# Deferring the factors and biases of five DeepNorms in a two-layer encoder trunk

## The chip, the core and the metric

One core of one Trainium2 chip. The metric is the device time of one execution in microseconds; times of several executions are given by their median. TensorE (PE in the profile, PEld for its weight loads) multiplies, VectorE (DVE), ScalarE (ACT) and GpSimd (POOL) work elementwise, SyncE (SP) issues most transfers. Each engine runs its own instructions in order and waits for the others by semaphores.

## The reference, cut to what matters

512 tokens of 1024 features go through two layers. Layer 0 is FFN, mLSTM mixer, FFN, embedding gate; layer 1 is FFN, gMLP mixer, FFN, embedding gate. After each of the eight parts stands a post-normalisation of `ALPHA * x + part`, over the features of a token:

```
def layer_norm(x, g, b):
    mu = jnp.mean(x32, axis=-1, keepdims=True)
    var = jnp.mean(jnp.square(x32 - mu), axis=-1, keepdims=True)
    y = (x32 - mu) * lax.rsqrt(var + LN_EPS) * g + b
...
x = layer_norm(DN_ALPHA * x + 0.5 * swiglu_ffn(x, ...), ln_g[i, 0], ln_b[i, 0])
x = layer_norm(DN_ALPHA * x + mix, ln_g[i, 1], ln_b[i, 1])
x = layer_norm(DN_ALPHA * x + 0.5 * swiglu_ffn(x, ...), ln_g[i, 2], ln_b[i, 2])
ple = jax.nn.sigmoid(x @ ple_wg[i] + ple_bg[i]) * (p[i] @ ple_wp[i])
x = layer_norm(DN_ALPHA * x + ple, ln_g[i, 3], ln_b[i, 3])
```

All of it is float32. The result is the normalised x of the last part.

## The kernel before

The state `xt` stands in the core's memory by tokens: four tiles t of 128 tokens with 1024 features each. Products need x by features, so each tile is turned: `turn_x` transposes it on PE in halves of four 128x128 blocks, ScalarE copies the half rounded to the short format (`xh`, line 419), and DVE subtracts to get the low part (`xl`, line 420). Every product is three matmuls, high times high, high times low and low times high (`mm3`, lines 250 to 254). Weights are split the same way: class `Weights` loads raw tiles through SP's queue, ScalarE makes `whi` (line 182) and DVE `wlo` (line 183), or GpSimd where a caller gives `low=pool`. A fixed order of all splits (`W.order`) is worked down as buffers come free: `release` gives one back and calls `fill`; with `later=True` it is only noted in `W.held`, and `refill` frees it. There are four buffers of the kind main; stages open more (`rows`, `extra`). `take` hands the next split tile to a product, and calls `refill` where none is ready.

The order of the work on each engine is the order of the program text. A stage ends with a `down` product: for each token tile t it adds into two PSUM banks (of four, `dn_bank`), over the n parts of the hidden state. Behind it DVE adds the result to `xt` (`residual`, lines 516 to 521: L519 for the first addition, which also scales by ALPHA, L521 for the others), takes the statistics (L500), and `Norm.apply` (lines 502 to 514) follows for the tile before, at k = 1 of the next tile. `apply` is: mean and variance (L505), plus eps (L507), GpSimd's power -0.5 (L508), and for each half of the features two scalar_tensor_tensor passes, subtract the mean and multiply by the factor (L511), multiply by the reciprocal deviation and add the bias (L512). The factor and bias stand in `g_bc` and `b_bc`, spread over all partitions. Tiles 0 and 1 are turned inside the down product (lines 548 and 549); tiles 2 and 3 in four hooks, which the next stage calls between its matmuls. The last hook (`last_turn`) also calls `W.refill(4)`.

The next stage starts with `up_staged` (lines 581 to 599) where it is an FFN or the mLSTM: three products over tokens 0 to 255 first, with the four hooks inside the second and third, then the same three over tokens 256 to 511, whose first product needs tiles 2 and 3. The gMLP starts with products by token tile (line 1047), with hooks ahead of and inside each, and takes four weight tiles for the first of them. In an FFN (`ffn`, line 665) the hidden features come in chunks of 2, 4, 4, 4, 4, 4 blocks; each block takes two steps i, a Silu (L701) and a product (L707). The first chunk's `down` stands at chunk 1, step 1 (line 715), with n = 2. In the mLSTM, value tiles are made by token tile (`project_v`, line 866), with the gates' scan (L801) and its transposes (L813, L815) between them. The embedding stage (`ffn_ple`, line 1134) computes a gate by tokens (lines 1186 to 1212) with the norm of each tile in `rest`.

Of the kernel before, what the change touches and what calls it, by code (L numbers as in the profile page):

```python
# [9 lines left out]
F32 = mybir.dt.float32  # L10
F32R = mybir.dt.float32r
AF = mybir.ActivationFunctionType
OP = mybir.AluOpType
# [208 lines left out]
def hybrid_trunk(ctx: ExitStack, tc, x, p, ln_g, ln_b, ffn1_wgu, ffn1_wd, ffn2_wgu, ffn2_wd,  # L222
# [188 lines left out]
    def turn_x(t, bank=dn_bank, halves=(0, 1)):  # L411

        for g in halves:
# [4 lines left out]
            dst = (slice(None), slice(4 * g, 4 * g + 4), slice(t * P, (t + 1) * P))  # L418
            sca.activation(xh[dst], ps, AF.Copy)
# [3 lines left out]
    NCOL = 160  # L423
# [3 lines left out]
    def load_columns():  # L427
# [6 lines left out]
                ("vn_b", gm_vn_b[0].rearrange("(a c) -> a c", c=P))]  # L434
# [52 lines left out]
    class Norm:  # L487
        def __init__(self, layer, k, out=None):
            self.out, self.st = out, {}
# [12 lines left out]
        def apply(self, t):  # L502
            y = xt[:, t]
# [5 lines left out]
            mean, rstd = mv[:, 0:1], rs[:, 1:2]  # L509
            for c in (slice(0, 512), slice(512, D)):  # L510
                vec.scalar_tensor_tensor(y[:, c], y[:, c], mean, self.g_bc[:, c], op0=OP.subtract, op1=OP.mult)  # L511
                vec.scalar_tensor_tensor(y[:, c], y[:, c], rstd, self.b_bc[:, c], op0=OP.mult, op1=OP.add)  # L512
                if self.out is not None:
                    nc.sync.dma_start(self.out[0, t * P:(t + 1) * P, c], y[:, c])

# [8 lines left out]
    hooks = []  # L524
# [5 lines left out]
    def last_turn():  # L530
        turn_x(TB - 1, halves=(1,))
        W.refill(4)

    def set_hooks():
        hooks.extend([lambda: turn_x(TB - 2, halves=(0,)), lambda: turn_x(TB - 2, halves=(1,)),
                      lambda: turn_x(TB - 1, halves=(0,)), last_turn])

    def down(hs, first, norm=None, low=None):

        n = len(hs)  # L540
        ws, kinds = [], []
        for t in range(TB):
            banks = [dn_bank("dps"), dn_bank("dps")]
            for k in range(n):
# [3 lines left out]
                if norm is not None and k in (1, 2) and t >= 2:  # L548
                    turn_x(t - 2, up_bank, (k - 1,))
                if norm is not None and k == 1 and t:  # L550
                    norm.apply(t - 1)
# [4 lines left out]
                if t == TB - 1:  # L556
                    kind = "rows" if kinds[k] == "rows" else None
                    if norm is None:
                        W.release(kind=kind, low=low)
                    elif kind == "rows":  # L560
                        W.free[kind] += 1
                    else:
                        W.release(later=bool(W.held), low=pool)
                        if not W.held:
                            W.held.append("none")
# [4 lines left out]
        if norm is not None:  # L570
            norm.apply(TB - 1)
            set_hooks()
# [92 lines left out]
    def ffn(layer, k, rows, prepare=None):  # L665
        with stage_pool("forms", 2) as fpool, stage_pool("quarters", Q_BUFS) as qpool, stage_pool("hpool", 2) as hpool:
# [16 lines left out]
            for c, n in enumerate(FFN_CHUNKS):  # L683
# [10 lines left out]
                for i in range(2 * n):  # L694
# [17 lines left out]
                    if group is not None and i < 7:  # L712
                        group.product(i)
                        group.form()
# [541 lines left out]
```

## Time and profile before

| | |
|---|---|
| median of 3 runs | 2289.18 us (2288.74 to 2290.45) |
| the profiled execution | 2285.76 us |
| its span, first to last instruction | 2284.0 us |
| PE busy | 2239.8 us |
| DVE busy | 1495.8 us |
| ACT busy | 784.2 us |
| POOL busy | 206.4 us |

The profile has times in us from the start of the span, durations of groups as a mean in ns. A wait is put down to the instruction that came last by the profile. PE's matmuls are pipelined, so the duration of one (about 0.39 us for 128x512) is longer than the step from one to the next. [...]

### The profile page before, as it was taken

What the parts mean: (1) busy time and instruction counts of PE and PEld (TensorE: products, weight loads), DVE (VectorE), ACT (ScalarE), POOL (GpSimd) and SP (SyncE); (2) the same over time, 40 slices, a digit from 0 to 9 for tenths busy, and PEclk for the clock granted to TensorE, in tenths of its full rate; (3) what the DMA queues carried; (4) which work ended last, traced back from release to release, by engine and by line L of the source; (5) the groups of instructions that cost most, each with busy time, mean ns of one, the idle gap of its engine ahead of it and who ended that gap; (6) DMA issues with size and microseconds to landing.
All of it is one profiled execution on the core that took longest, in us unless ns stands there. A gap on an engine that the chain in (4) does not pass through costs nothing.

```text
span 2284.0 us, 26044 instructions
## 1 busy us (share of the span) xinstructions
PE 2239.8 (98%) x10622; PEld 1873.3 (82%) x10622; DVE 1495.8 (65%) x2093; ACT 784.2 (34%) x1032; POOL 206.4 (9%) x143
## 2 busy tenths in 40 slices
PE   8999999999999999999999999999999999999997
PEld 7888888887878788888878888888888888888886
DVE  4566659676666656666687566668566674666677
ACT  3333333442534123333243233333333332333332
POOL 1000002132232300000010000001021210000010
PEclk9999999999999999999999999999999999999999
DMA  7332222133231333331332333222322243332212
GB/s 232 113 98 86 93 86 95 48 114 110 66 102 56 120 111 120 111 96 62 111 120 88 112 105 111 93 70 95 131 93 86 75 133 113 129 111 83 83 65 74
DMA packets 172848, 228.30 MB, mean 100 GB/s; under 512 B 4788, under 2 KB 130836, under 8 KB 172728
## 3 DMA queue, kind: packets, MB, share of 16 engines
q1 hardware_dynamic: 165824, 211.83, 28.6%
q10 hardware_dynamic: 6616, 14.69, 2.0%
q8 instruction: 83, 1.36, 0.2%
q14 instruction: 37, 0.30, 0.0%
q0 software_dynamic: 288, 0.12, 0.0%
HBM read 224.51 MB, written 2.11 MB: 99 GB/s over the span
## 4 chain that ended last, share of the span: by engine, by line
PE 82%; DVE 12%; issue 2%; POOL 2%; ACT 1%; DMA 1%; POOLq 0%; SPq 0%; ACTq 0%; DVEq 0%
PE fps L253 13%; PE fps L254 13%; PE fps L252 13%; PE gps L253 4%; PE gps L254 4%; PE gps L252 4%; PE dps L253 3%; PE dps L254 3%; PE dps L252 3%; DVE wlo L183 2%; DVE xt L512 2%; DVE st L500 1%; PE gups L252 1%; PE vps L252 1%; PE gups L253 1%
## 5 line engine op out<-in xcount | busy, mean ns | idle before, releaser
L252 PE MATMUL fps<-xh,whi 128*128 128x512 f32 x1312 | 510.6, 389 | 0.0
L253 PE MATMUL fps<-xl,whi 128*128 128x512 f32 x1312 | 510.4, 389 | 0.0
L254 PE MATMUL fps<-xh,wlo 128*128 128x512 f32 x1312 | 510.4, 389 | 0.0
L183 DVE TENSOR_TENSOR wlo<-wraw,whi 128x1024 fp32r<-128x1024 f32 (+1 forms) x274 | 336.0, 1242 | 199.2 <-ACT whi L182 197.4
L182 ACT ACTIVATE whi<-wraw 128x1024 fp32r<-128x1024 f32 (+1 forms) x333 | 344.1, 1048 | 263.3 <-PE dps L254 126.2
L252 PEld LDWEIGHTS fps<-xh,whi 128*128 128x128 f32 x1312 | 246.3, 188 | 51.1
L254 PEld LDWEIGHTS fps<-xh,wlo 128*128 128x128 f32 x1312 | 246.3, 188 | 51.0
L253 PEld LDWEIGHTS fps<-xl,whi 128*128 128x128 f32 x1312 | 246.3, 188 | 50.9
L183 DVE TENSOR_TENSOR wlo<-wquarter,whi 128x1024 fp32r<-128x1024 f32 x112 | 137.2, 1225 | 201.9 <-ACT whi L182 201.9
L182 ACT ACTIVATE whi<-wquarter 128x1024 fp32r<-128x1024 f32 x112 | 118.7, 1059 | 238.0 <-PE gps L254 177.8
L183 POOL TENSOR_TENSOR wlo<-wraw,whi 128x1024 fp32r<-128x1024 f32 x59 | 151.8, 2581 | 278.5 <-ACT whi L182 247.4
L254 PE MATMUL gps<-whi,flo 128*128 128x512 f32 x448 | 174.3, 389 | 0.0
L252 PE MATMUL gps<-whi,fhi 128*128 128x512 f32 x448 | 174.3, 389 | 0.0
L253 PE MATMUL gps<-wlo,fhi 128*128 128x512 f32 x448 | 174.3, 389 | 0.0
L508 POOL TENSOR_TENSOR rs<-rs,eps_pow 128x1 f32<-128x1 f32 x32 | 30.3, 947 | 1542.7 <-DVE rs L507 1538.3
L701 ACT ACTIVATE sg<-fps 128x512 f32<-128x512 f32 x80 | 47.9, 598 | 279.1 <-PE fps L254 279.1
L521 DVE TENSOR_TENSOR xt<-xt,gps 128x512 f32<-128x512 f32 x224 | 143.2, 680 | 0.0
L253 PE MATMUL dps<-wlo,hh 128*128 128x512 f32 x256 | 101.6, 397 | 9.5 <-DVE wlo L183 9.5
L257 ACT ACTIVATE fhi<-h 128x512 fp32r<-128x512 f32 x112 | 69.5, 625 | 116.2 <-DVE h L637 45.8
L252 PE MATMUL dps<-whi,hh 128*128 128x512 f32 x256 | 101.9, 398 | 1.8 <-ACT hh L257 1.8
L254 PE MATMUL dps<-whi,hl 128*128 128x512 f32 x256 | 101.4, 396 | 1.7 <-DVE hl L258 1.7
L258 DVE TENSOR_TENSOR flo<-h,fhi 128x512 fp32r<-128x512 f32 x112 | 75.7, 688 | 36.4 <-ACT fhi L257 36.4
(266 smaller groups left out, 3909.6 us busy)
## 6 DMA issues: line engine op xcount, KB each, us to landing
wraw<-in_ffn_wgu_dram SPq DMA_DIRECT2D x80, 1024.0 KB, 5.3
wquarter<-in_ffn_wd_dram SPq DMA_DIRECT2D x64, 512.0 KB, 3.8
wraw<-in_ml_w_in_dram SPq DMA_DIRECT2D x24, 1024.0 KB, 5.4
wraw<-in_gm_w_in_dram SPq DMA_DIRECT2D x15, 1024.0 KB, 5.8
wraw<-in_ffn_wd_dram SPq DMA_DIRECT2D x12, 1024.0 KB, 5.0
wraw<-in_ml_w_out_dram SPq DMA_DIRECT2D x8, 1024.0 KB, 5.0
wraw<-in_ple_wg_dram SPq DMA_DIRECT2D x8, 1024.0 KB, 5.1
wraw<-in_gm_w_out_dram SPq DMA_DIRECT2D x8, 1024.0 KB, 4.9
```

The lines of the kernel that those rows point to most:

```text
L182: self.nc.scalar.activation(hi[:, s], src[:, s], AF.Copy)
L183: (low or self.nc.vector).tensor_sub(lo[:, s], src[:, s], hi[:, s].bitcast(F32))
L252: mm(ps, st[0], mv[0], start=start, stop=False, skip_group_check=more)
L253: mm(ps, st[0], mv[1], start=False, stop=False, skip_group_check=more)
L254: mm(ps, st[1], mv[0], start=False, stop=stop, skip_group_check=more)
L257: sca.activation(hi, src, AF.Copy)
L258: vec.tensor_sub(lo, src, hi.bitcast(F32))
L500: vec.bn_stats(self.st[t][:, i], xt[:, t, i * D // n:(i + 1) * D // n])
L508: pool.tensor_tensor(rs[:, 1:2], rs[:, 0:1], eps_pow, op=OP.pow)
L512: vec.scalar_tensor_tensor(y[:, c], y[:, c], rstd, self.b_bc[:, c], op0=OP.mult, op1=OP.add)
L521: vec.tensor_add(dst, dst, ps)
L701: sca.activation(sg, ps, AF.Silu)
```

## The change

Five of the eight norms become deferred: those behind the first FFNs, the mixers and the first embedding gate (`k != 2`, and not the last of the kernel). A deferred norm only centres and scales by the reciprocal deviation, in one tensor_scalar over 1024 features. The factors and biases are applied twice. By features, when the tile is turned: four ScalarE Identity instructions with per-partition scale and bias write a tile `xf`, from which `xh` and `xl` are made. And by tokens, for the residual path: `finish`, two DVE passes over a tile, called through `run_affine` in the next stage: in an FFN at chunk 0 step 3 (tile 0), chunk 1 step 0 (tile 1) and chunk 1 step 1 (tiles 2 and 3, ahead of `down`); in the mLSTM behind each value tile; in the gMLP from the last token tile of the first column block on.

`apply` is cut into `prepare` (to the power) and `scale`; in `down` the first half-turn of tile t-2 stands between the two, and so does the second where the norm isn't deferred. Buffers of the first three weight tiles of a down product with a norm are released together at k = 2, with the low part on DVE; behind a first FFN the release is only noted (`lazy`). The embedding gate's releases no longer name GpSimd. The column table grows from 160 to 288 columns, with three more small loads on GpSimd's queue and one more transpose. The gMLP's statistics tile moves to another pool.

```
-    def turn_x(t, bank=dn_bank, halves=(0, 1)):
+    def turn_x(t, bank=dn_bank, halves=(0, 1), norm=None):
...
+            if norm is not None and norm.deferred:
+                xf = tmp_tile("xf").rearrange("p (k c) -> p k c", k=4)
+                for k in range(4):
+                    sca.activation(xf[:, k], ps[:, k], AF.Identity, scale=col("ln_g", norm.at + 4 * g + k),
+                                   bias=col("ln_b", norm.at + 4 * g + k))
+                ps = xf
             sca.activation(xh[dst], ps, AF.Copy)
             vec.tensor_sub(xl[dst], ps, xh[dst].bitcast(F32))
...
-    NCOL = 160
+    NCOL = 288
...
+                ("ln_g", ln_g.rearrange("l k (a c) -> (l k a) c", c=P)),
+                ("ln_b", ln_b.rearrange("l k (a c) -> (l k a) c", c=P))]
...
+            self.deferred = out is None and k != 2
...
+        def scale(self, t):
+            y = xt[:, t]
+            mean, rstd = self.rs[t]
+            if self.deferred:
+                vec.tensor_scalar(y, y, mean, rstd, op0=OP.subtract, op1=OP.mult)
+                return
...
+        def finish(self, t):
+            vec.tensor_mul(xt[:, t], xt[:, t], self.g_bc)
+            vec.tensor_add(xt[:, t], xt[:, t], self.b_bc)
...
+    def run_affine(n=1):
+        for _ in range(n):
+            if affine:
+                affine.pop(0)()
...
+        if norm.deferred:
+            affine.extend([lambda t=t: norm.finish(t) for t in range(TB)])
...
+            elif kind == "rows":
+                W.free[kind] += 1
+            else:
+                W.release(later=lazy or bool(W.held))
...
-                if norm is not None and k in (1, 2) and t >= 2:
-                    turn_x(t - 2, up_bank, (k - 1,))
                 if norm is not None and k == 1 and t:
-                    norm.apply(t - 1)
+                    norm.prepare(t - 1)
+                    if t >= 2:
+                        turn_x(t - 2, up_bank, (0,), norm)
+                        if not norm.deferred:
+                            turn_x(t - 2, up_bank, (1,), norm)
+                    norm.scale(t - 1)
+                if norm is not None and k == 2 and t >= 2 and norm.deferred:
+                    turn_x(t - 2, up_bank, (1,), norm)
...
-                        W.release(later=bool(W.held), low=pool)
...
+                    if norm is None or k > 2:
+                        release(kinds[k])
+                    elif k == 2:
+                        for kind in kinds[:3]:
+                            release(kind)
...
+                    if (c, i) in ((0, 3), (1, 0), (1, 1)):
+                        run_affine(2 if (c, i) == (1, 1) else 1)
                     if i == 1 and pending is not None:
                         down(pending, True)
...
-            down(pending, False, norm)
+            down(pending, False, norm, lazy=prepare is None)
...
                         between[t]()
+                    run_affine()
...
-            st = mp.tile([P, TB, 4, 6], F32, name="gst")
+            st = tmp.tile([P, TB, 4, 6], F32, name="gst", tag="pad", bufs=3)
...
+                    if (c, t) >= (0, TB - 1):
+                        run_affine()
...
-                    W.release(later=bool(W.held) or last, low=pool)
+                    W.release(later=bool(W.held) or last)
```

## Rows read from the trace of the kernel before

**Rows 1.** The page, part 1: busy us, share of the span, instructions.
```profile
PE 2239.8 (98%) x10622; PEld 1873.3 (82%) x10622; DVE 1495.8 (65%) x2093; ACT 784.2 (34%) x1032; POOL 206.4 (9%) x143
```

**Rows 2.** The waits of PE: who waited for whom: us, times, longest.
```profile
PE xps L417 <- DVE xt L512: 4.1, 1, 4.1
PE sup L596 <- DVE xl L420: 3.4, 2, 2.4
```

**Rows 3.** Windows of edges 1 to 5, PE alone: stretch, us, busy, clock, DMA.
```profile
365.80:378.10 12.30, 9.88 (x84) 1.00 0.37 108
797.99:808.88 10.89, 9.90 (x83) 1.00 0.01 2
1215.10:1230.59 15.49, 11.39 (x84) 0.89 0.22 68
1573.74:1591.00 17.26, 15.94 (x78) 1.00 0.35 107
1858.60:1868.62 10.02, 9.90 (x84) 1.00 0.46 159
```

**Rows 4.** A window inside edge 3: PE, PEld, DVE, ACT, POOL busy, then the clock.
```profile
1227.00:1230.30 3.30, 3.30 (x17) 3.30 (x17) 2.95 (x5) 0.60 (x1) 0.00 (x0) 0.50 0.00 0
```

**Rows 5.** The timeline of POOL and DVE at edges 4 and 3: start, us, instruction.
```profile
1575.22 2.41 POOL L183 TENSOR_TENSOR wlo<-wraw,whi 128x1024 fp32r<-128x1024 f32 x1 [1.45 <-ACT whi L182]
...
1575.26 2.93 DVE L512 SCALAR_TENSOR_TENSOR xt<-xt,rs,b_bc 128x512 f32<-128x512 f32 x1
...
1218.57 2.10 DVE L1203 TENSOR_TENSOR pg<-pg,pw 128x256 f32<-128x256 f32 x1
```

**Rows 6.** Groups by line and shape: count, busy us, mean ns, idle before.
```profile
L511 DVE SCALAR_TENSOR_TENSOR xt<-xt,mv,g_bc 128x512 f32<-128x512 f32 x64 | 47.6, 744 | 0.0
...
L508 POOL TENSOR_TENSOR rs<-rs,eps_pow 128x1 f32<-128x1 f32 x32 | 30.3, 947 | 1542.7 <-DVE rs L507 1538.3
...
L1062 DVE TENSOR_SCALAR gvf<-gvf,gmv,grs 128x2048 f32<-128x2048 f32 x4 | 5.4, 1346 | 2.9 <-POOL grs L1061 2.9
...
L507 DVE TENSOR_SCALAR rs<-mv 128x1 f32<-128x1 f32 x32 | 4.9, 154 | 1.1
...
L183 DVE TENSOR_TENSOR wlo<-wquarter,whi 128x1024 fp32r<-128x1024 f32 x112 | 137.2, 1225 | 201.9 <-ACT whi L182 201.9
...
L887 ACT ACTIVATE sz<-zps,cols 128x512 f32<-128x512 f32 x16 | 11.0, 689 | 52.8 <-PE zps L254 52.7
...
L701 ACT ACTIVATE sg<-fps 128x512 f32<-128x512 f32 x80 | 47.9, 598 | 279.1 <-PE fps L254 279.1
...
L914 ACT ACTIVATE ex<-rbc,reach 128x128 f32<-128x128 f32 x24 | 8.2, 387 | 0.0
```

**Rows 7.** The timeline of ACT in the mLSTM: three small activations in a row.
```profile
424.27 0.97 ACT L914 ACTIVATE ex<-rbc,reach 128x128 f32<-128x128 f32 x3
```

**Rows 8.** Layer 1's first FFN, chunk 1: DVE's timeline, then PE's window of `dps`.
```profile
1256.61 0.69 DVE L707 SCALAR_TENSOR_TENSOR h<-sg,fps 128x512 f32<-128x512 f32 x1 [2.58 <-PE fps L254]
1257.53 1.23 DVE L183 TENSOR_TENSOR wlo<-wraw,whi 128x1024 fp32r<-128x1024 f32 x1 [0.24 <-ACT whi L182]
1258.68 1.34 DVE L519 SCALAR_TENSOR_TENSOR xt<-xt,dps 128x512 f32<-128x512 f32 x2
...
1256.40:1261.85 5.45, 5.44 (x25) 4.51 (x25) 1.82 (x3) 1.00 0.73 229
```

**Rows 9.** The mLSTM's gates: DVE's timeline, then PE's.
```profile
411.84 0.68 DVE L876 TENSOR_TENSOR vf<-vps,vb 128x512 f32<-128x512 f32 x1
...
413.86 1.20 DVE L801 TENSOR_TENSOR_SCAN mrow<-frow,irow_s 4x512 f32<-4x512 f32 x1
...
415.56 0.41 PE L815 MATMUL mcol<-ident,mrow 4*128 4x4 f32 x4
```

**Rows 10.** The page, part 6: issues, KB each, median us to landing.
```profile
wraw<-in_ml_w_in_dram SPq DMA_DIRECT2D x24, 1024.0 KB, 5.4
```

More of the change, by code (lines that the diff above doesn't have):

```diff
@@ L433, in load_columns @@
                 ("vn_g", gm_vn_g[0].rearrange("(a c) -> a c", c=P)),
-                ("vn_b", gm_vn_b[0].rearrange("(a c) -> a c", c=P))]
+                ("vn_b", gm_vn_b[0].rearrange("(a c) -> a c", c=P)),
+                ("ln_g", ln_g.rearrange("l k (a c) -> (l k a) c", c=P)),
+                ("ln_b", ln_b.rearrange("l k (a c) -> (l k a) c", c=P))]
         at, tiles = 0, []
@@ L488, in __init__ @@
         def __init__(self, layer, k, out=None):
-            self.out, self.st = out, {}
+            self.out, self.st, self.rs = out, {}, {}
+            self.deferred = out is None and k != 2
+            self.at = (layer * 4 + k) * KB
             self.g_bc = act.tile([P, D], F32, name="g_bc", tag="g_bc")
@@ L500, in stats, with prepare @@
             vec.bn_stats(self.st[t][:, i], xt[:, t, i * D // n:(i + 1) * D // n])
-        def apply(self, t):
-            y = xt[:, t]
+        def prepare(self, t):
             mv = small.tile([P, 2], F32, name="mv", tag="mv")
@@ L508, in apply @@
             pool.tensor_tensor(rs[:, 1:2], rs[:, 0:1], eps_pow, op=OP.pow)
-            mean, rstd = mv[:, 0:1], rs[:, 1:2]
+            self.rs[t] = mv[:, 0:1], rs[:, 1:2]
+        def scale(self, t):
[4 more added lines that the diff above has]
+                return
             for c in (slice(0, 512), slice(512, D)):
@@ L514, in apply @@
                     nc.sync.dma_start(self.out[0, t * P:(t + 1) * P, c], y[:, c])
+        def apply(self, t):
+            self.prepare(t)
+            self.scale(t)
+        def finish(self, t):
+            vec.tensor_mul(xt[:, t], xt[:, t], self.g_bc)
+            vec.tensor_add(xt[:, t], xt[:, t], self.b_bc)
     def residual(t, half, ps, first):
@@ L521, in residual @@
             vec.tensor_add(dst, dst, ps)
-    hooks = []
+    hooks, affine = [], []
     def run_hook():
@@ L528, in run_hook, with set_hooks, turn, last_turn @@
             hooks.pop(0)()
[L530 to L538, printed above, removed]
+    def run_affine(n=1):
+        for _ in range(n):
+            if affine:
+                affine.pop(0)()
+    def set_hooks(norm):
+        def turn(t, half):
+            return lambda: turn_x(t, halves=(half,), norm=norm)
+        def last_turn():
+            turn(TB - 1, 1)()
+            W.refill(4)
+        hooks.extend([turn(TB - 2, 0), turn(TB - 2, 1), turn(TB - 1, 0), last_turn])
+        if norm.deferred:
+            affine.extend([lambda t=t: norm.finish(t) for t in range(TB)])
+    def down(hs, first, norm=None, low=None, lazy=False):
         n = len(hs)
         ws, kinds = [], []
+        def release(kind):
+            kind = "rows" if kind == "rows" else None
+            if norm is None:
+                W.release(kind=kind, low=low)
+            elif kind == "rows":
+                W.free[kind] += 1
+            else:
+                W.release(later=lazy or bool(W.held))
+                if not W.held:
+                    W.held.append("none")
         for t in range(TB):
@@ L556, in down @@
                 if t == TB - 1:
[L557 to L562, printed above, removed]
-                        W.release(later=bool(W.held), low=pool)
-                        if not W.held:
-                            W.held.append("none")
+                    if norm is None or k > 2:
[3 more added lines that the diff above has]
+                            release(kind)
             for half, ps in enumerate(banks):
@@ L571, in down @@
             norm.apply(TB - 1)
-            set_hooks()
+            set_hooks(norm)
     def up(ps, w, t0=0, t1=SEQ, hooked=()):
@@ L1191, in ffn_ple @@
                         ps = dn_bank("gps")[:, :m]
-                        turn = (lambda: turn_x(t - 2, up_bank)) if t >= 2 and e == 0 and not last else None
+                        turn = (lambda: turn_x(t - 2, up_bank, norm=norm)) if t >= 2 and e == 0 and not last else None
                         up_tokens(t, ws[half], ps, slice(e * m % 512, e * m % 512 + m), turn,
@@ L1215, in ffn_ple @@
                 if not last:
-                    set_hooks()
+                    set_hooks(norm)
     turn_x(0)
```

## The prediction

> **What bounds the kernel now.** I read the page first: TensorE (PE) is busy for 98% of the span [rows 1], so the change can win only where PE waits and lose only where it makes PE wait. The waits of PE come next [rows 2]: 4.1 us on the last normalised tile, 3.4 us on the turned low parts xl, all at the edges between stages, where a DeepNorm stands between the last down product of one stage and the first product of the next. Then one window for each of the five edges whose norm becomes deferred, from the first matmul of the new stage to its last transpose [rows 3]. I number them by time: 1 into the mLSTM, 2 into its second FFN, 3 from the layer embedding into layer 1, 4 into the gMLP, 5 into the last FFN. All but edge 4 hold the same 66 half-width matmuls and 16 transposes. Edge 5 needs 10.02 us, edge 1 12.30, edge 2 10.89, edge 3 15.49; so edge 5 is the measure of one that waits for little, and the others stand 2.3, 0.9 and 5.5 us above it. Edge 4 has 17.26 us with 15.94 busy: 1.3 idle. [...] In sum 10.0 us stand to be won, 0.4% of the run.
>
> What makes VectorE (DVE) late there is seen in single instructions: while GpSimd forms a low part in 2.41 us, a DVE instruction that starts beside it takes 2.93 or, at half the width, 2.10 us [rows 5], where the first pass of a norm over the same width takes 0.74 [rows 6].
>
> **What goes.** A norm of one 128-token tile was four passes, close to 0.70 us apart, of which the first runs under GpSimd's power (0.95) [rows 6]: 3.3 us from the first pass to the end. Now it is the power and then one tensor_scalar of 128x1024. That form stands in the trace at 2048 columns, 1346 ns, and at one column, 154 ns [rows 6]; halfway between, it is 0.75 us. A deferred norm so ends about 1.4 us sooner. The stretch of 1.7 to 2.2 us goes with GpSimd's low part; at edges 2, 3 and 5 a DVE low part of 1.23 us [rows 6] stands in its place, at edges 1 and 4 the split is put off. Edges 1 and 2 lose their excess: 2.3 and 0.9 us. At edge 3 DVE is behind PE in all four tiles, and I go down its list: 3 x 1.4 us sooner, then 1.5 us in which it waits for the whi of the split (ScalarE makes that only behind a sigmoid) and 1.2 us for the low part, less the stretch. The last statistics come 3.2 us sooner, the last transposes 3.3; about 0.95 us of the wait stays, too short for the clock to fall, as the waits of edge 1 go by at 1.00 [rows 3]. That wins 5.5 - 0.95 = 4.5. Edge 4 wins its 1.3. **Won: 9.0 us.** The two edges behind a second FFN (norm not deferred) also lose a stretched instruction, but the one exposed wait on L512 [rows 2] is that of edge 3, so I take nothing.
>
> **What comes, 1: ScalarE in the turn.** Each half of a turn gains four 128x128 Identity pieces ahead of the Copy, each with two per-feature operands. The trace has no such piece. One operand costs 0.09 us (689 ns with one, 598 without, both 128x512 from PSUM), and 128x128 with one takes 387 ns [rows 6]; three in a row take 0.97 [rows 7], so they start 0.29 apart. With the second operand at the same 0.09, a piece is 0.48 long and starts 0.38 after the one before: 3 x 0.38 + 0.48 = 1.6 us, bounds 1.25 (the second is free) and 1.9 (no overlap). The Copy behind them keeps its 0.6. In the old order the last xl is ready about 0.7 us ahead of its use: 18 half-width matmuls at half of 5.45/24 us [rows 8] are 2.05 us, less the Copy and a DVE pass of 0.68. So 1.6 - 0.7, about 1.0 us with the hand-offs, is exposed at each of edges 1, 2, 3 and 5 (edge 4 goes tile by tile and hides it): **4.0 us**, bounds 1.2 and 6.4. [...]
>
> **2: the factor and bias passes ahead of an FFN's first down product.** They are `finish`, two DVE tensor_tensor of 128x1024 at 1.23 us [rows 6], 2.4 us a tile, 9.7 an edge. With tiles 0 and 1 nothing is lost: DVE has gaps there. Tiles 2 and 3 are queued at chunk 1, step 1, right ahead of `down(pending, True)`, whose residual adds stand behind them on DVE. Now DVE runs L707, the low part at 1257.53 and the first residual add at 1258.68 [rows 8]. With four passes between, 4.8 us, that add starts at 1263.4 and ends at 1264.1. PE has four banks for this product and fills two per tile of 12 matmuls: after two tiles, 24 matmuls or 5.45 us [rows 8] (the row counts the next one too), it must have the first bank back, at 1261.9. It waits 2.2 us. Edges 2, 3 and 5 lead into an FFN: **6.6 us**, bounds 5.7 and 7.5.
>
> **3: the same passes in the mLSTM.** Tile 0's passes stand between the two value tiles that DVE works off without pause (the second at 411.84), with the gate scan behind (413.86 + 1.20); PE transposes the scan's result 0.5 us after the scan ends [rows 9]. The scan comes 2.4 us later, and up to 1.2 more because the put-off split adds a third low part ahead of the convolution. I take **2.6 us**, bounds 0 (if DVE has caught up by then) and 3.6. Tiles 1 to 3 and the gates' way through DRAM lie beside the last value tile and the z products. In the gMLP each tile's 2.4 us fits into a period of 5.45.
>
> **4: the put-off split at edge 4.** The gMLP's first product takes four tiles at once, and the fourth was GpSimd's, done at 1577.63 [rows 5], just ahead of PE. Now `take` finds three, and the split is made there: DVE comes to it only behind the residual, statistics and norm of tile 3, about 1579.4, and ends at 1580.6; PE wants it at 1578.1. **2.4 us**, bounds 0 and 3. At edges 1 and 4 the load that follows the split goes later by the same, 1 MB on SP's queue that lands 5.4 us after its issue [rows 10]; two more tiles are split before its own is wanted, and PE takes over 1.3 us with each, so I count nothing for it, at most 1.
>
> **5: the start.** Three more small loads on the GpSimd queue and one transpose: the loads are issued some 15 us ahead of their use; nothing to 0.2, I take 0.
>
> **The sum.** -9.0 + 4.0 + 6.6 + 2.6 + 2.4 = +6.6 us. It is made on the profiled execution (span 2284.0, 2285.76 with what lies around it); the median of the runs stands 3.42 us above that, and the same difference goes with it: 2289.18 + 6.6 = 2295.8. About 0.2%, 4.6 us, is what a measurement of this kernel can tell from no change.
>
> **Rivals.** *The moved work is covered* (ends on the other side): the passes fall into DVE's idle third, and TensorE finds xl in time. Decided at the first residual add of each FFN: if it isn't later than 1261.9 in the old clock, nothing is lost. Then only the 9.0 won remain: 2280.2. For it: DVE is idle for a third of the span. Against it: an engine in order can't use that idle time behind the wait for L707 [rows 8]. Chance 0.14. *Only the FFN pays*: the gate rows, the fourth tile and the turn are ready in time, which takes a ScalarE piece at its low bound and a DVE that has caught up; -9.0 + 6.6 = -2.4, so 2286.8, no change. Chance 0.24. *The small ScalarE pieces pay in full*: 0.3 us more per half, 0.6 for the two halves at the end of a turn, four edges: +2.4, 2298.2. [...] Chance 0.08. *The clock falls in the new waits*: 3.3 us at 0.50 cost 1.65 each [rows 4]; at the three FFNs and the gate rows, +6.6: 2302.4. Against it: the clock held at edge 1, whose single wait was as long. Chance 0.08. The forecast keeps 0.46, with a range of its own of 2290 to 2299.
>
> **How the numbers follow.** The range has to take in the forecast's own and the case in which only the FFN pays; 2285 to 2299.5 leaves out the covered case and the clock's, 2 in 10. Faster by over 0.2% (under 2284.6): the covered case and a little of the second, 0.14 + 0.04 = 0.18. Within 0.2%: most of the second (0.20) and the lower part of the forecast's range (0.10), 0.30. Slower: the rest of the forecast (0.36) and the last two, 0.52.
>
> **What would show it.** Right: the long DVE instructions at the edges are gone, edge 1's window is near 11 us and edge 3's near 12, with the clock at 1.00; PE has three waits of about 2.2 us on the residual add (L519 before) inside the first down product of the FFNs behind edges 2, 3 and 5, one ahead of the scan's transposes, and one on a wlo in the gMLP's first tile. Wrong: if those down products run through their 48 matmuls without a wait, the second part falls; if an Identity piece is under 0.40 us, the first shrinks; if edge 3 keeps over 3 us of waiting, the gain is smaller than I have it; if the fourth tile is ready when the gMLP begins, the fourth part falls.

## The result and the profile after

The changed kernel takes 2297.14 us (median of 8 runs, 2292.56 to 2298.43); the kernel before, on the same chip, 2288.72 (8 runs). The ratio is 1.0034 [1.0025, 1.0043]: 8.4 us slower, where 6.6 were forecast. The profiled execution is the fastest of the eight, 2292.56 us with a span of 2290.8, 6.8 above the span before.

The page of the changed kernel, part 1, answers [rows 1]; under it the waits of PE, which answer [rows 2] (us, times, longest; lines that the kernel before has too are left out).

```profile
PE 2242.9 (98%) x10623; PEld 1875.4 (82%) x10623; DVE 1502.7 (66%) x2080; ACT 843.6 (37%) x1192; POOL 182.4 (8%) x139
```

```profile
PE dps L252 <- DVE xt L545: 6.6, 3, 2.2
...
PE brow L864 <- DVE gt L848: 2.8, 1, 2.8
PE sup L253 <- DVE xl L426: 2.5, 8, 0.3
...
PE gvps L253 <- DVE wlo L183: 1.9, 1, 1.9
...
PE mcol L866 <- DVE mrow L852: 0.5, 1, 0.5
```

The 4.1 and 3.4 us of [rows 2] are gone. Five rows that were not there before take their place: the residual add in three FFNs, the gates of the mLSTM (two rows), the turned low parts, eight times, and a weight's low part in the gMLP. The windows of the edges, cut as in [rows 3] (stretch, us, busy, clock, DMA):

```profile
366.00:375.85 9.85, 9.85 (x85) 1.00 0.08 28
801.87:811.72 9.85, 9.85 (x85) 1.00 0.01 2
1220.27:1230.13 9.86, 9.86 (x86) 1.00 0.34 106
1578.30:1596.19 17.89, 15.99 (x78) 1.00 0.51 163
1863.56:1873.41 9.85, 9.85 (x85) 1.00 0.45 161
```

Up to their last transpose edges 1, 2, 3 and 5 now run without a pause, in 9.85 us instead of 12.30, 10.89, 15.49 and 10.02; edge 4 has grown. So the change does at the edges what it says, and pays behind them. The place of one of its largest payments, DVE in layer 1's first FFN, answers [rows 8]:

```profile
1257.01 0.69 DVE L756 SCALAR_TENSOR_TENSOR h<-sg,fps 128x512 f32<-128x512 f32 x1 [0.18 <-PE fps L254]
1257.93 1.23 DVE L183 TENSOR_TENSOR wlo<-wraw,whi 128x1024 fp32r<-128x1024 f32 x1 [0.24 <-ACT whi L182]
1259.08 1.22 DVE L539 TENSOR_TENSOR xt<-xt,g_bc 128x1024 f32<-128x1024 f32 x1
1260.33 1.22 DVE L540 TENSOR_TENSOR xt<-xt,b_bc 128x1024 f32<-128x1024 f32 x1
1261.47 1.22 DVE L539 TENSOR_TENSOR xt<-xt,g_bc 128x1024 f32<-128x1024 f32 x1
1262.72 1.22 DVE L540 TENSOR_TENSOR xt<-xt,b_bc 128x1024 f32<-128x1024 f32 x1
1263.86 2.47 DVE L545 SCALAR_TENSOR_TENSOR xt<-xt,dps 128x512 f32<-128x512 f32 x4
```

Four passes stand between the low part and the first residual add, which so starts at 1263.86; the matmul that needs its bank was due at 1262.2. PE stops there, and the clock falls behind it. Two windows of PE, in this product and behind the gate rows:

```profile
1264.50:1271.70 7.20, 7.10 (x24) 0.76 0.04 1
418.00:424.95 6.95, 6.95 (x25) 0.75 0.01 4
```

In each lies a stretch of 3.41 us in which the granted clock was 0.50; the one at edge 3 [rows 4] is gone.

**A ledger.** All kernels below run the same 10,623 matmuls and transposes in the same order (before: one transpose fewer), so two traces can be laid on each other: the start of a matmul in the one less its start in the other, taken ahead of a stretch and behind it, is what the stretch costs more. The base is a kernel of the experiments, the one with three placements and without the pieces, whose PE waits at no edge; it leaves out the factors and biases by features, so it computes something else and serves for times alone. The columns are the kernel before, the changed kernel, the experiment with three placements and the kernel of the last experiment. Microseconds above the base, from one profiled execution of each:

| stretch | before | changed | three placements | the last kernel |
|---|---|---|---|---|
| edge 1 | 2.75 | 1.15 | 1.15 | 0.77 |
| the mLSTM's gates | 0.00 | 5.16 | 0.00 | 1.20 |
| edge 2 and the FFN's first down | 1.30 | 3.64 | 1.16 | 0.75 |
| the two embedding stages | 2.30 | 0.10 | 0.85 | 0.06 |
| edge 3 and the FFN's first down | 5.85 | 5.25 | 1.15 | 0.77 |
| edge 4 | 1.82 | 2.22 | 0.00 | 0.00 |
| the gMLP behind it | 0.03 | 0.00 | 1.82 | 0.00 |
| edge 5 and the FFN's first down | 0.46 | 3.64 | 1.16 | 0.76 |
| all else | -0.47 | -0.32 | 2.54 | 1.19 |
| sum | 14.04 | 20.84 | 9.83 | 5.50 |

### The profile page after: what moved, and what is told of

Its sections match the earlier page's. It is cut to its first block, busy times and chain, and to the rows that moved or that the text cites. A ratio compares the mean times of both kernels' runs of the same rounds, so it can differ in the third digit from the quotient of the medians.

```text
span 2290.8 us, 26172 instructions
## 1 busy us (share of the span) xinstructions
PE 2242.9 (98%) x10623; PEld 1875.4 (82%) x10623; DVE 1502.7 (66%) x2080; ACT 843.6 (37%) x1192; POOL 182.4 (8%) x139
## 4 chain that ended last, share of the span: by engine, by line
PE 88%; DVE 7%; ACT 2%; issue 1%; DMA 1%; POOL 1%; SPq 0%; POOLq 0%; DVEq 0%; ACTq 0%
PE fps L253 13%; PE fps L252 13%; PE fps L254 13%; PE gps L253 5%; PE gps L254 5%; PE gps L252 5%; PE dps L254 4%; PE dps L253 4%; PE dps L252 4%; PE gups L252 1%; DVE wlo L183 1%; PE gups L253 1%; PE gups L254 1%; PE gvps L253 1%; PE gvps L254 1%; PE gvps L252 1%
## 5 line engine op out<-in xcount | busy, mean ns | idle before, releaser
L183 DVE TENSOR_TENSOR wlo<-wraw,whi 128x1024 fp32r<-128x1024 f32 (+1 forms) x281 | 344.3, 1241 | 188.0 <-ACT whi L182 186.1
L183 POOL TENSOR_TENSOR wlo<-wraw,whi 128x1024 fp32r<-128x1024 f32 x52 | 134.3, 2592 | 269.5 <-ACT whi L182 234.4
L519 POOL TENSOR_TENSOR rs<-rs,eps_pow 128x1 f32<-128x1 f32 x32 | 20.6, 644 | 1578.5 <-DVE rs L518 1578.5
```

The source lines that it names most:

```text
L183: (low or self.nc.vector).tensor_sub(lo[:, s], src[:, s], hi[:, s].bitcast(F32))
L519: pool.tensor_tensor(rs[:, 1:2], rs[:, 0:1], eps_pow, op=OP.pow)
```

## The experiments

**The passes ahead of the first down product.**

```
-                    if (c, i) in ((0, 3), (1, 0), (1, 1)):
-                        run_affine(2 if (c, i) == (1, 1) else 1)
+                    if (c, i) in ((0, 3), (1, 0)):
+                        run_affine()
...
                     norm.stats(t, half, 2)
+            if norm is None:
+                run_affine()
```

> The changed kernel with one thing moved: in an FFN, the factor and bias passes of tiles 2 and 3 no longer stand ahead of the first down product but behind the residual adds of its tiles 0 and 1. My theory (the four passes hold up the first residual add): TensorE's three waits of 2.35 us on that add go, 7.05 us in all, and with them the half-clock stretch behind the second one, some 1.7 us; against the kernel before the time is then between -0.5 and +1.4 us, a ratio near 1.0002 where the changed kernel had 1.0034. A rival says that the loss comes from the split of the low parts on VectorE and would only move: then the waits come back at the next residual add or at a wlo, and the ratio stays near 1.003. Half way (the passes now delay the second pair of residual adds by 1 us each): 1.0015.

Measured: 2285.76 us, ratio 0.9990 [0.9981, 0.9999]. The wait on L545 is not among PE's waits any more, and the same part of layer 1's FFN runs through; PE's window of it in this kernel (stretch, us, busy, clock, DMA):

```profile
1258.00:1266.00 8.00, 8.00 (x37) 1.00 0.47 156
```

The passes were the cause, and their place alone turns a loss of 8.4 us into a gain of 2.7. That is 11 us by the medians, more than the waits of 7.05 and one half-clock stretch. In the ledger the three stretches fall from 3.64, 5.25 and 3.64 to 1.16 each, 9.1 us. The two profiled executions differ by 5.0 us only: the changed kernel's is its fastest of eight, this one the second slowest of eleven, and in it the gates, edge 4 and the start cost 0.6, 1.6 and 1.2 us more, at a mean granted clock of 0.995 where the changed kernel's has 0.996. That the changed kernel's other runs have more half-clock stretches than its profiled one fits their clock (below), but no trace of them shows it.

**The gate rows.** The first try moved all four tiles' passes.

```
-                    run_affine()
+                    if t == 2:
+                        run_affine()
...
                 ss = scores(h, qk, rt)
+                run_affine()
...
                 hn = mix(h, ss, v)
+                run_affine(2)
```

> The changed kernel with the mLSTM's factor and bias passes moved: none between the value tiles ahead of the gate scan; one tile's behind the third value tile, one behind the scores, two behind the mix. My theory (tile 0's passes delay the gate scan): the waits on the gate rows (3.0 and 0.5 us beyond a matmul's own spacing) go, with the half-clock stretch behind them about 1.7 more: 3.5 to 5.2 us less than the changed kernel, a ratio of 1.0012 to 1.0019 against the kernel before. The rival, that the scan is late because the put-off split adds a low part ahead of the convolution: the waits stay at 1 us or more, and the ratio is 1.0025 or above.

Measured: 2299.90 us, ratio 1.0054 [1.0041, 1.0066], slower than the changed kernel, as neither theory had it. The wait on the gate rows did fall, to 0.4 us, but the last two tiles' passes now stood ahead of four low parts that the next head's first product needs. One of the passes took 3.39 us besides, where the two behind it took 1.21 and 1.22. PE's wait (us, times, longest) and DVE's timeline (start, us, instruction) in this kernel:

```profile
PE qps L254 <- DVE wlo L183: 5.9, 1, 5.9
```

```profile
457.26 3.39 DVE L540 TENSOR_TENSOR xt<-xt,b_bc 128x1024 f32<-128x1024 f32 x1
460.57 1.21 DVE L539 TENSOR_TENSOR xt<-xt,g_bc 128x1024 f32<-128x1024 f32 x1
461.82 1.22 DVE L540 TENSOR_TENSOR xt<-xt,b_bc 128x1024 f32<-128x1024 f32 x1
462.96 4.62 DVE L183 TENSOR_TENSOR wlo<-wraw,whi 128x1024 fp32r<-128x1024 f32 x4
```

The experiment made the mistake of the FFN once more, at another place. The second try moved tile 0 alone: `if t:` ahead of the `run_affine()` between the value tiles, and one `run_affine()` behind the scores.

> The changed kernel with only tile 0's factor and bias passes in the mLSTM moved: not ahead of the gate scan but behind the scores; tiles 1 to 3 keep their places behind the value tiles. My theory (two causes in one wait): the wait on the gate rows falls by these passes' 2.4 us, from 2.96 to about 0.6 us, the 0.56 us behind it stays with the put-off split, and no new wait comes at the q product, since nothing stands ahead of its low parts any more. That is 2.4 us, and up to 1.7 more if the half-clock stretch behind the wait goes: a ratio of 1.0017 to 1.0024 against the kernel before, where the changed kernel had 1.0034. The rival (these passes must be paid somewhere in the mLSTM, as the last try showed): the wait only moves again, and the ratio stays at 1.003 or above.

Measured: 2292.17 us, ratio 1.0016 [1.0006, 1.0025]. PE's waits on the gates in this kernel:

```profile
PE mcol L866 <- DVE mrow L852: 0.5, 1, 0.5
PE brow L864 <- DVE gt L848: 0.4, 1, 0.4
```

The first theory holds in its number and its two causes: 5.16 us in the ledger became 1.16, and no new wait came. (The profiled execution is as long as the changed kernel's even so: half-clock stretches at edge 4 and in the FFN behind edge 5 took 1.6 us each, at a mean granted clock of 0.995.) The 1.16 that stay go with the put-off split: the kernel that also makes the split at once has 0.00. They come back in the kernels with more VectorE instructions per turn (the last column), where the split isn't put off. That reads as if a lead of about a microsecond were lost to any addition ahead of the convolution; no run tests it by itself.

**The put-off split.** `down(pending, False, norm)` without `lazy`.

> The changed kernel with the split at the end of a last down product made at once on VectorE instead of being put off until the next stage takes the tile (this bears on the edge into the mLSTM and the edge into the gMLP). My theory: the wait of 2.06 us on the fourth wlo in the gMLP's first product goes, and the gate scan comes up to 0.6 us sooner; 2.1 to 2.7 us less than the changed kernel, a ratio near 1.0024 against the kernel before. The rival, that the low part made at once delays the last statistics and norm by its own 1.2 us at both edges: the edge windows grow by up to 1.2 us each and the ratio stays at 1.0030 to 1.0035.

Measured: 2291.82 us, ratio 1.0016 [1.0007, 1.0025]. The theory's waits shrank (gMLP's first product from 2.22 to 0.00, the gates from 5.16 to 2.29 with the clock), but 2.6 us came back in the gMLP, 2.1 of them at the first spatial product. Edge 1 stays at 1.17, so the rival's delay isn't there. The ledger's sum falls by 2.3 us, as the theory had it; the ratio falls by 0.0018, 4.1 us, more than it had. The first of DVE's waits of 1600 to 1670 us in this kernel (us, times, longest):

```profile
DVE gvf L1105 <- DMA gvb<-in_gm_b_in_dram: 10.5, 3, 4.3
```

DVE stands there three times for a bias row whose load is issued on ScalarE's queue behind the last Gelu of the chunk before. The last experiment takes this up.

**The pieces.** The first of two runs left them out of the changed kernel (`if False:` in place of the test in `turn_x`).

> The changed kernel without ScalarE's four Identity pieces in each half of a turn: the factors and biases by features are left out of the turned x behind the five deferred norms (those by tokens stay). My theory: the four pieces delay the last turned low part, and the waits on xl of 0.33 and 0.42 us at four edges go: 3.0 us less than the changed kernel, a ratio near 1.0021 against the kernel before. The rival, that these waits are set by VectorE's own pass behind ScalarE and not by the pieces: the waits stay, under 1 us is won, and the ratio is 1.003 or above. If the small pieces paid in full, the gain would be nearer 5 us and the ratio 1.0012.

Measured: 2289.16 us, ratio 1.0005 [0.9996, 1.0014]: about 8 us less by the medians, not 3. The waits on xl went, so the rival falls, 4.6 us in the ledger; 1.0 at edge 4 went too, and which waits are followed by a half-clock stretch changed, so this run can't price the pieces. The second one does, below.

**The low part alone.** In the kernel before, `low=pool` is taken out at the same two places as by the change, and nothing else.

> The kernel before with one thing of the change alone: the low part at the end of a last down product and in the embedding's products is made by VectorE and not by GpSimd; the norms stay as they were. My theory (a third to a half of the 9.0 us that I had as won is the stretch of a VectorE instruction beside GpSimd): 2 to 4 us less than before, a ratio of 0.9982 to 0.9991, with the waits on the last normalised tile of edges 1 and 3 shorter by 1 us or more. The rival, that the low part of 1.23 us on VectorE takes back what the stretch cost: the same or slower, 1.000 or above, and the gain of the change at the edges is then all the shorter norm's.

Measured: 2289.36 us, ratio 1.0003 [0.9994, 1.0012]: the rival. PE's waits on the norm and on xl in this kernel are longer than in [rows 2], 10.1 instead of 7.5 us:

```profile
PE xps L417 <- DVE xt L512: 5.6, 2, 4.8
PE sup L596 <- DVE xl L420: 4.5, 3, 2.9
```

By the ledger edges 1 and 4 and the two embedding stages win 1.0, 1.1 and 2.2 us, and edges 2, 3 and 5 lose 2.0, 0.7 and 1.1. At edges 2 and 5 the low part on DVE (1.21 us, from 796.07 and 1855.70) stands ahead of a norm and holds it up.

**Three placements at once**: three of the edits above together (the FFN's passes, tile 0 behind the scores, the split at once).

> The changed kernel with three placements at once: tiles 2 and 3 behind the residual adds in the FFN, tile 0 behind the scores in the mLSTM, and the split at the end of a last down product made at once. If the single effects add up (11.4, 2.4 to 4 and 5 us off the changed kernel's 8.4 us above the kernel before), the time is 10.4 to 12 us below the kernel before, a ratio of 0.9948 to 0.9955. The rival, that they share the same half-clock stretches and the same DVE backlog ahead of the gate scan: about 6 us below, a ratio near 0.9975.

Measured: 2281.52 us, ratio 0.9973 [0.9962, 0.9983]: it beats both kernels, by the rival's number. The ledger says why the single gains don't add: no edge and no gate is worse than the pieces' 1.16, but 1.82 us come in the gMLP, 1.4 of them at the spatial product, and a half-clock stretch, 1.9 us, in the first down product of the mLSTM.

**GpSimd again**, in that kernel: `low=pool` in both places.

> The kernel with the three placements, and GpSimd's low part back at the end of a last down product and in the embedding's products; the norms stay short. The last try of this kind (the kernel before without GpSimd's low part) came out the same, since the edges then waited for the low part of 1.2 us on VectorE. Theory A (the two parts of the gain need each other: the shorter norm wins only where no VectorE instruction is stretched beside GpSimd): a VectorE instruction of 2 us or more stands at each edge again, TensorE waits 1 to 2 us at three or more of the five edges, and the time is 3 to 7 us above the kernel with the three placements, a ratio of 0.9985 to 1.0005 against the kernel before. Theory B (the shorter norm alone holds the whole gain, and GpSimd's part can be on either engine): within 1.5 us of the kernel with the three placements, 0.997 to 0.998.

Measured: 2282.28 us, ratio 0.9971 [0.9959, 0.9982]: theory B. The stretch is back, as the timeline of POOL and DVE ahead of edge 3 shows (start, us, instruction), but PE's window of the edge below it has no pause:

```profile
1213.10 2.42 POOL L183 TENSOR_TENSOR wlo<-wraw,whi 128x1024 fp32r<-128x1024 f32 x1 [3.86 <-ACT whi L182]
...
1213.71 2.08 DVE L1261 TENSOR_TENSOR pg<-pg,pw 128x256 f32<-128x256 f32 x1
```

```profile
1215.50:1226.00 10.50, 10.50 (x91) 1.00 0.28 100
```

So what the change wins at the edges it wins with either engine; where the low part is made is worth nothing that can be measured. The short norm is the likeliest cause: by the prediction's estimate it ends 1.4 us sooner in each tile. But no run has it without the other things that the change does in the same place, such as the turn between `prepare` and `scale` and the release of three weight tiles together, so its share isn't shown.

**The pieces' price**, in the kernel with the three placements.

> The kernel with the three placements, without ScalarE's four pieces in each half of a turn: the factors and biases by features are left out of the turned x behind the five deferred norms (those by tokens stay). Theory A (the pieces cost what the waits on xl show, 0.75 us at each of four edges): the eight waits on xl go, and the time is 3.0 us below the kernel with the three placements, a ratio near 0.996 against the kernel before. Theory B (they cost more, as the 8 us of the first try without them suggest, where part was the clock): 5 us or more below it, 0.995 or lower. If another wait takes their place: less than 1.5 us.

Measured: 2272.95 us, ratio 0.9933 [0.9920, 0.9947], 8.6 us below the kernel with the pieces: theory B by its number. The ledger, of which this run is the base, splits the 9.8 us between the two profiled executions: 1.16 at each of four edges, 4.6; 1.8 in the gMLP; 1.9 in the mLSTM's first down product, with the clock (a mean of 0.998 in this execution, 0.996 in the other); 0.85 in the embedding stages; the rest at the start. Only the 4.6 are shown to be the pieces' own: the kernel of the last experiment keeps the pieces and has neither the 1.8 nor the 1.9. And the waits on xl are all of the 1.16, not 0.75 of it. Matmul by matmul they hold PE for 0.44 and 0.53 us, and the matmul behind each for 0.10; the 0.33 and 0.42 were counted with the step of a full-width matmul, 0.23 us, where these have 0.12.

**Pieces on two engines.**

```
+                    if k % 2 and bank is dn_bank:
+                        vec.tensor_scalar(xf[:, k], ps[:, k], gk, bk, op0=OP.mult, op1=OP.add)
+                    else:
+                        sca.activation(xf[:, k], ps[:, k], AF.Identity, scale=gk, bias=bk)
```

> The kernel with the three placements, and in the turns that run between the first products of a stage every second one of the four factor-and-bias pieces on VectorE (tensor_scalar from PSUM) instead of ScalarE. My theory (ScalarE's row of four pieces sets when the last turned low part is ready): the waits on xl of 0.33 and 0.42 us at four edges go, 1.5 to 3 us less than the kernel with the three placements. The rival, that VectorE's pieces stand in order behind its residual adds and low parts and make the turn no earlier: no difference, or up to 1 us slower.

Measured: 2305.47 us, ratio 1.0070 [1.0057, 1.0082], 24 us worse than without. Neither theory has that size, but the rival's mechanism is there: PE waits for xh, and ScalarE's waits at edge 3, in the second fence, show for whom it waits in turn. The third has ScalarE's longest wait and, from DVE's timeline, what DVE did until then.

```profile
PE sup L252 <- ACT xh L428: 13.9, 4, 3.8
```

```profile
ACT xf L426 <- DVE xf L424: 5.3, 4, 3.1
ACT xh L428 <- DVE xf L424: 1.9, 4, 0.5
```

```profile
1230.40 0.46 ACT L426 ACTIVATE xf<-xps,cols 128x128 f32<-128x128 f32 x1 [3.08 <-DVE xf L424]
...
1229.23 0.81 DVE L529 TENSOR_SCALAR xt<-xt,mv,rs 128x1024 f32<-128x1024 f32 x1 [0.73 <-POOL rs L522]
1229.96 0.40 DVE L424 TENSOR_SCALAR xf<-xps,cols 128x128 f32<-128x128 f32 x1
```

Two things add up. DVE's first piece of an edge stands in order behind the last tile's residual, statistics and norm, and ScalarE, which has made its own first piece, waits 3.1 us for it (3.5 at edge 1). Then the two engines write different blocks of one tile `xf`, and each piece waits for the other engine's piece before it, so a half takes 2.65 us where ScalarE alone takes 2.1.

**Halves.** In the turns between the first products, two pieces, their Copy and DVE's subtraction, then the other two.

```
+                    if k % 2 and bank is dn_bank:
+                        half = (slice(None), slice(4 * g + k - 1, 4 * g + k + 1), dst[2])
+                        sca.activation(xh[half], xf[:, k - 1:k + 1], AF.Copy)
+                        vec.tensor_sub(xl[half], xf[:, k - 1:k + 1], xh[half].bitcast(F32))
+                if bank is dn_bank:
+                    continue
```

> The kernel with the three placements, and in the turns that run between the first products of a stage ScalarE makes two pieces and their Copy, then the other two and theirs, with VectorE's low part behind each Copy at half the width. Laid matmul by matmul beside the kernel that left the pieces out, the kernel with the three placements loses 1.16 us at each of four edges. My theory (the first turned low part is late because it stands behind all four pieces and a Copy of the full width): its wait of 0.42 us and the small ones behind it go, 2.5 to 4.6 us in all, a time of 2277 to 2279 us and a ratio near 0.996 against the kernel before. The rival, that what counts is the end of the whole chain, which is now longer by two short instructions on each engine: no gain, or up to 1.5 us slower than the kernel with the three placements.

Measured: 2280.06 us, ratio 0.9956 [0.9943, 0.9970], not told apart from the kernel without it. At the edges it does what the theory says at half the size: 1.16 became 0.75, and no wait on xl is long enough any more to stand among PE's waits. ScalarE's timeline at edge 1 (start, us, instruction):

```profile
376.10 0.79 ACT L422 ACTIVATE xf<-xps,cols 128x128 f32<-128x128 f32 x2
376.92 0.42 ACT L426 ACTIVATE xh<-xf 128x256 fp32r<-128x256 f32 x1
377.25 0.79 ACT L422 ACTIVATE xf<-xps,cols 128x128 f32<-128x128 f32 x2
378.07 0.42 ACT L426 ACTIVATE xh<-xf 128x256 fp32r<-128x256 f32 x1
```

ScalarE hands on the first two blocks after 1.2 us, not all four after 2.1. The profiled execution is the slowest of the five (2285.17 us; the others 2278.50 to 2280.49): in it 5.4 us come in the gMLP, at a weight's low part, at the spatial product and with the clock (a mean of 0.995, in the others 0.998).

**The late bias row.** In that kernel the row of the next chunk is loaded behind the first token tile of a chunk (in the first chunk behind the third).

```
+                    if c < 3 and t == (0 if c else 2):
+                        nvb = bias_row(c + 1)
```

> The kernel with the three placements and the turned low parts by halves, and in the gMLP each bias row of the value half is loaded one to three tiles earlier. In the kernels that gain time ahead of the gMLP, TensorE waits 1 to 2 us on the first spatial product again; VectorE there stood 4 to 5 us for a bias row that is issued only behind the last Gelu of the chunk before. My theory (this late row gives back what the earlier split won): VectorE's three waits on it, 11 us in all, shrink to 2 us or less, the wait on the spatial product and the half-clock stretch behind it go, 1.8 to 3.5 us less than with the halves alone, 2276 to 2278.5 us and a ratio near 0.9948. The rival, that the four low parts ahead of the last tile on VectorE set it: the waits on the row go, the wait at the spatial product stays, and the time is the same within 1 us.

Measured: 2277.24 us, ratio 0.9946 [0.9932, 0.9960]. The first two of DVE's waits of 1600 to 1660 us in this kernel; the row is not among them, and PE has no wait on the spatial product:

```profile
DVE gst L1121 <- ACT gvf L1120: 7.7, 11, 0.7
DVE gvf L1119 <- PE gvps L254: 5.2, 4, 2.8
```

In the gMLP 5.4 us became 0.0, so the late row was what gave back the gain of the split made at once. It does so only together with the pieces: in the base of the ledger DVE waits 7.5 us for the same row, and PE doesn't wait at the spatial product. By its median this is the fastest kernel of the study that computes everything, 11.6 us below the kernel before; from the one with the halves alone its ratio is not told apart.

## Why the prediction was right

By edge, as the prediction's own terms add up there, against the ledger (changed less before):

| stretch | forecast | measured |
|---|---|---|
| edge 1 | -2.3 + 1.0 = -1.3 | -1.60 |
| the gates | +2.6 | +5.16 |
| edge 2, FFN | -0.9 + 1.0 + 2.2 = +2.3 | +2.34 |
| embedding stages | 0 | -2.20 |
| edge 3, FFN | -4.5 + 1.0 + 2.2 = -1.3 | -0.60 |
| edge 4 | -1.3 + 2.4 = +1.1 | +0.40 |
| edge 5, FFN | +1.0 + 2.2 = +3.2 | +3.18 |
| all else | 0 | +0.15 |
| sum | +6.6 | +6.80 |

The sum is right in part by luck. In this table two errors of over 2 us, at the gates and in the embedding stages, cancel. By the terms the luck is larger: what was won is 14.4 us and not 9.0, and what came (parts 1 to 4) is 21.1 and not 15.6, so errors of over 5 us on either side cancel. The mechanisms, below, are the named ones, but for what made DVE late.

**Part 2** (6.6) carried the forecast and held: three waits of 2.2 us on L545, the add at 1263.86 where 1263.4 was worked out. In the ledger a wait costs 2.49, with the small gaps beside it, and the half-clock stretch behind the second 1.6 more: 9.1 us in all, above the part's upper bound of 7.5. That the passes' place is the cause is shown by the first experiment.

**Part 1** (4.0) measured 4.6. The piece was cheaper than the 0.48 us estimated, four in 1.49 us instead of 1.6; so the lead of 0.7 us that was set against it was smaller, about 0.3 by the same working (1.49 less 1.16). The windows of edges 1 and 3 didn't come out near 11 and 12 us, as the prediction's signs had it, but at 9.85, since these waits stand behind the last transpose, where the windows end. Groups of the changed kernel (busy us and mean ns behind the bar), and in the second fence ACT's timeline of its last half-turn at edge 1:

```profile
L422 ACT ACTIVATE xf<-xps,cols 128x128 f32<-128x128 f32 x160 | 59.9, 454 | 55.9 <-PE xps L417 55.9
...
L519 POOL TENSOR_TENSOR rs<-rs,eps_pow 128x1 f32<-128x1 f32 x32 | 20.6, 644 | 1578.5 <-DVE rs L518 1578.5
L526 DVE TENSOR_SCALAR xt<-xt,mv,rs 128x1024 f32<-128x1024 f32 x20 | 16.2, 811 | 8.4 <-POOL rs L519 8.4
```

```profile
376.08 1.49 ACT L422 ACTIVATE xf<-xps,cols 128x128 f32<-128x128 f32 x4
377.61 0.63 ACT L425 ACTIVATE xh<-xf 128x512 fp32r<-128x512 f32 x1
```

That four pieces fit into 1.49 us rules out the rival in which small pieces pay in full, 1.9 us for four.

**Part 3** (2.6) is the first mis-sized term. The mechanism was the named one: tile 0's passes stand ahead of the scan, as DVE's timeline of the changed kernel shows.

```profile
411.98 1.22 DVE L539 TENSOR_TENSOR xt<-xt,g_bc 128x1024 f32<-128x1024 f32 x1
413.23 1.23 DVE L540 TENSOR_TENSOR xt<-xt,b_bc 128x1024 f32<-128x1024 f32 x1
414.38 0.68 DVE L927 TENSOR_TENSOR vf<-vps,vb 128x512 f32<-128x512 f32 x1
...
416.30 0.16 DVE L848 COPY gt<-gsum 128x16 f32<-128x16 f32 x1
416.38 1.20 DVE L852 TENSOR_TENSOR_SCAN mrow<-frow,irow_s 4x512 f32<-4x512 f32 x1
```

PE's first transposes of the gates wait for the copy at 416.30 behind these. But the "up to 1.2 more" of the put-off split came in full (1.16), and a half-clock stretch that cost 1.6 followed, which the term had left to a rival: its upper bound of 3.6 was right for the waits (2.96 + 0.58, matmul by matmul) and not for the time.

**Part 4** (2.4) measured 2.22; edge 4 won 1.8 instead of 1.3.

**Won** (9.0) is the second mis-sized term, and the largest: 14.4 us in the ledger. Edge 3 kept none of the 0.95 us that was left standing; each edge had 0.35 to 0.5 us of small waits that the measure, edge 5, had as well; and the two edges behind a second FFN, at which the prediction took nothing because no exposed wait had a row there, gave 2.2. Before, DVE's second pass at the first of them ran beside GpSimd's low part (timelines of POOL and DVE in the kernel before):

```profile
1153.12 2.40 POOL L183 TENSOR_TENSOR wlo<-wraw,whi 128x1024 fp32r<-128x1024 f32 x1
...
1153.10 2.98 DVE L512 SCALAR_TENSOR_TENSOR xt<-xt,rs,b_bc 128x512 f32<-128x512 f32 x1 [0.44 <-POOL rs L508]
...
1156.78 0.75 DVE L512 SCALAR_TENSOR_TENSOR xt<-xt,rs,b_bc 128x512 f32<-128x512 f32 x1
```

So the pass took 2.98 us beside the low part's 2.40, against 0.75 alone; what makes it longer is not shown.

**What makes DVE late** was explained wrongly: the prediction named the stretch beside GpSimd, though most of what it had as won at edge 3 came from the shorter norm (3 x 1.4 us). The experiment on the low part alone (1.0003) takes the stretch away and wins nothing, and the one that brings it back loses nothing. With or without it, the four passes a tile in the old order came too late at the edges. Only at the embedding stages, whose norms the change leaves long, does taking the low part off GpSimd win by itself, 2.2 us; put back into the kernel with the three placements it costs 0.5 there (1.34 against 0.85 in the ledger).

**The rivals.** That the moved work is covered fell at the first residual add. That only the FFN pays fell at the gate rows and in the gMLP. "The clock falls in the new waits" came true in part and beside the forecast: in the profiled execution behind two of the five new waits of 2 us or more, at 1.6 us each. The clock also fits the median's distance from the profiled execution: two of the eight runs have a mean granted clock of 0.996 and 2293.6 us on average, six have 0.994 and 2297.5. A mean lower by 0.002 over 2290 us is 9.2 us at half the rate, of which 4.6 are lost; 3.9 were measured. The kernel before has its median 3.0 us above its profiled execution, the changed kernel 4.6; this difference is why the median stands at +8.4 and the profiled execution at +6.8. The prediction had taken it to be the same.

**Open:** why one wait of 2.2 us is followed by a half-clock stretch and the next like it is not. No run here tells it.

## What to carry to other kernels

Work moved off a busy edge has to be put behind the instruction that hands a buffer back, not ahead of it: the same four passes, at three places, cost 9 us in the ledger on one side of a residual add and nothing on the other. Look for the first consumer on the in-order queue, and for every other queue that stands there; one of the moves here made a new wait of 5.9 us. An average of idle time (DVE's third) said nothing about it here. And when a fix wins less than its wait, lay the two traces on each other by matmul: the gain given back shows where it is.

## What was not expected of the hardware

- GpSimd's power of 128x1 took 0.55 us where DVE waits for it, and 0.92 where a DVE pass runs beside it: the mean fell from 947 [rows 6] to 644 ns, a gain of 0.4 us for a tile of a deferred norm that the sum didn't have.
- A turned half made in two parts was later to finish (2.4 us instead of 2.2) and earlier to hand on its first blocks (1.2 us), and here PE's wait hung on those: 1.16 us at an edge became 0.75.
- Each of the five half-clock stretches ahead of the tail, in the traces of the kernel before and of the changed kernel, is 3.41 us long and begins 3.1 to 5.3 us behind the start of a wait of PE. In the ledger those at the gates and in layer 1's first FFN cost 1.6 us each. At edge 3, where the wait of 4.1 us was taken away, its stretch went (1.00 in the window above), and in the changed kernel two stood behind waits of 2.8 and 2.2 us that the kernel before doesn't have.
